# First layer of a hybrid decoder trunk: the opening reads a feature-major copy of x, and the first half's values get their token factor on the way out

## The chip, the cores and the metric

The kernel runs on one core of one Trainium2 chip. Its metric is the device time of one execution in microseconds (us), lower is better. The core has five engines that each work through their own instructions in order: TensorE (PE in the profile, its weight loads PEld), VectorE (DVE), ScalarE (ACT), GpSimd (POOL) and SyncE (SP), which issues most transfers.

## The reference

Two layers on 1024 tokens of 1024 features, all in f32. Cut to what matters here:

```python
def rmsnorm(x, g):
    y = x * lax.rsqrt(jnp.mean(x * x, axis=-1, keepdims=True) + RMS_EPS)
    return y * g

for l in range(DEPTH):                        # DEPTH = 2
    h = rmsnorm(x, norm1[l])
    proj = h @ w_in[l]                        # 1024 x 5120
    qa, ka, va, qb, kb, vb, gate_pre = jnp.split(proj, splits, axis=-1)
    o_a = dilated_mixture(qa, ka, va)         # 12 heads of sliding windows
    o_b = stick_breaking_attention(qb, kb, vb)   # 4 heads, causal
    gates = sigmoid(gate_pre + b_gate[l])
    merged = g_a * (o_a @ w_br[l, :256]) + g_b * (o_b @ w_br[l, 256:])
    x = x + merged @ w_o[l]
    ...                                       # a gated feed-forward with a 3-tap convolution
return rmsnorm(x, norm_f)
```

The normalized `h` is x times a factor for each token (one over the root of its mean square) times a gain for each feature.

## The kernel before

All activations lie feature-major in the on-chip memory: a tile has 128 features on its partitions and tokens along its rows. There are eight feature blocks (`KD`) and two halves of 512 tokens (`n`). Each f32 operand of a product is split into two parts, `hi` and `lo` (`hh`, `hl` for the normalized h, `w_hi`, `w_lo` for weights): ScalarE rounds to `hi`, VectorE subtracts to get `lo`, and TensorE does three matmuls, hi x hi, hi x lo and lo x hi (`product`, lines 188 to 190). The arguments of a matmul name its stationary operand and then its moving one.

The first layer opens with `first` (from line 2020) and `head` (from line 618). `first` reads x by token tiles of 128 tokens (`load`), squares them on ScalarE with a sum along the row, takes the root and the reciprocal (`scaled`), and turns each tile feature-major by eight TensorE transposes (`turned`, line 2054). The first two token tiles are scaled before they are turned (`in_two`); the other six are turned raw, copied out by ScalarE (`kept`, which also stores them to the DRAM tile `xs`), and scaled by eight VectorE instructions of 128 tokens, with the token factors spread over the partitions by another transpose (`normed`). The raw normalized h (`RAW`, `h_raw`) stays for later sums. `head` projects the stick-breaking values (`v_ps`, 256 columns of weights), keys (`kq_ps`) and queries (`q_ps`).

Behind the opening come the dense products of the layer (`i_a`, `i_b`, `i_c`), each over four feature blocks, in a fast-multiplication scheme that works on sums of quarters: `block_sums` (from line 1065) lets VectorE form these operand sums (`h_sum`, `h_raw`, line 1082 to 1091) and their splits (`t_hi`, `t_lo`), and for each weight tile the sums `in_a` and splits. Between them stand the attention items. One stick-breaking item (`stick_item`, line 707) has score matmuls `z`, ScalarE sigmoids `beta` and `stay`, a running product `stay` on VectorE (line 744), the product `beta` (line 751), transposes of `beta` on TensorE (`sb_t`, line 759) and matmuls with the values (`sb_o`).

TensorE's instructions stand in the order in which the program is written. In the opening ScalarE's and VectorE's order is written out too for the first steps, and left to the scheduler behind them, which orders instructions by its own estimates. Each engine then keeps its order: an instruction that waits holds all behind it on its engine. SP holds transfers in the same way.

## Time and profile before

| | us |
|---|---|
| median of 3 runs | 2603.27 |
| lowest to highest | 2602.32 to 2603.33 |
| the profiled execution | 2603.86 |
| its span on the core | 2602.2 |
| TensorE busy in the span | 2589.6 |
| VectorE busy | 2084.7 |
| ScalarE busy | 1349.5 |
| GpSimd busy | 105.6 |

Rows of a timeline give the start from the span's start, the time taken, engine, line, operation, output and inputs, shapes, and how many instructions in a row were merged; in brackets stands the idle time of the engine just before and what ended it. Instructions of one engine overlap at their ends, so the spacing of starts says more than the time of one. A row by stretches gives the busy time of each engine.

The opening's places in time: the first value matmul at 8.36, the first key matmul at 29.19, the first dense product at 65.39, the first score matmul of an attention item at 76.41.

### The profile page before, as it was taken

The numbers are of one execution on the slowest core, as the hardware profiler recorded it, in microseconds if no ns is written. First come the engines' busy times: TensorE is split into PE (matmuls) and PEld (weight loads), VectorE is DVE, ScalarE is ACT, GpSimd is POOL, SyncE is SP. The second block draws the span as 40 slices with busy tenths as digits, with TensorE's granted clock in tenths as the row PEclk, the third lists the DMA queues.
The fourth block names the chain that finished last, engine by engine and source line by source line (L and its number), as shares of the span: only waits on it lengthen the run. The fifth ranks groups of instructions, "written<-read, shape, count | busy, mean of one in ns | idle before, by whom it ended". The sixth has DMA issues, their size and how long they took to land.

```text
span 2602.2 us, 36060 instructions
## 1 busy us (share of the span) xinstructions
PE 2589.6 (100%) x12647; PEld 2165.4 (83%) x12647; DVE 2084.7 (80%) x3485; ACT 1349.5 (52%) x2521; POOL 105.6 (4%) x145
## 2 busy tenths in 40 slices
PE   9999999999999999999999999999999999999999
PEld 8888888888888888888888888888888888888887
DVE  8877777796888888897677788777869888889965
ACT  6555666664554545422445555666645555554225
POOL 3000000030000000000000000000300000000000
PEclk9999999999999999999999999999999999999999
DMA  7434578863244454688344436798633354447863
GB/s 257 152 119 134 163 207 226 236 235 101 88 148 157 138 176 134 243 325 311 146 147 146 128 127 194 194 235 238 198 99 121 122 171 136 154 162 264 342 242 118
DMA packets 401409, 470.60 MB, mean 181 GB/s; under 512 B 24500, under 2 KB 315980, under 8 KB 399436
## 3 DMA queue, kind: packets, MB, share of 16 engines
q1 hardware_dynamic: 400364, 465.90, 55.2%
q0 software_dynamic: 704, 2.13, 0.4%
q8 instruction: 100, 1.64, 0.3%
q14 instruction: 81, 0.66, 0.1%
q10 hardware_dynamic: 160, 0.27, 0.0%
HBM read 305.59 MB, written 162.63 MB: 180 GB/s over the span
## 4 chain that ended last, share of the span: by engine, by line
PE 93%; DVE 3%; ACT 2%; DMA 1%; issue 1%; SPq 0%; POOL 0%; DVEq 0%; ACTq 0%
PE u_a L1060 6%; PE u_a L1061 6%; PE u_a L1059 6%; PE d_ps L1823 5%; PE d_ps L1825 5%; PE d_ps L1824 5%; PE i_a L1059 5%; PE i_a L1060 5%; PE i_a L1061 5%; PE u_c L1059 3%; PE u_c L1060 3%; PE u_c L1061 3%; PE i_c L1059 2%; PE i_c L1061 2%; PE i_c L1060 2%; PE o_ps L188 2%
## 5 line engine op out<-in xcount | busy, mean ns | idle before, releaser
L146 ACT CAST w_hi<-up_a 128x512 fp32r<-128x512 f32 x280 | 174.0, 622 | 277.1 <-DVE up_a L1677 120.8
L154 DVE TENSOR_TENSOR w_lo<-up_a,w_hi 128x512 fp32r<-128x512 f32 x280 | 189.3, 688 | 83.6 <-ACT w_hi L146 83.6
L146 ACT CAST w_hi<-in_a 128x512 fp32r<-128x512 f32 x252 | 156.2, 622 | 161.8 <-PE i_c L1060 35.6
L154 DVE TENSOR_TENSOR w_lo<-in_a,w_hi 128x512 fp32r<-128x512 f32 x252 | 172.7, 687 | 73.3 <-ACT w_hi L146 64.7
L1834 DVE TENSOR_TENSOR x<-x,d_ps 128x512 f32<-128x512 f32 x220 | 149.9, 683 | 60.3 <-PE d_ps L1825 57.0
L1059 PE MATMUL u_a<-hh,w_hi 128*128 128x512 f32 x320 | 124.5, 389 | 0.0
L1060 PE MATMUL u_a<-hl,w_hi 128*128 128x512 f32 x320 | 124.5, 389 | 0.0
L1061 PE MATMUL u_a<-hh,w_lo 128*128 128x512 f32 x320 | 124.5, 389 | 0.0
L1059 PE MATMUL u_a<-t_hi,w_hi 128*128 128x512 f32 x320 | 124.5, 389 | 0.0
L1060 PE MATMUL u_a<-t_lo,w_hi 128*128 128x512 f32 x320 | 124.5, 389 | 0.0
L1061 PE MATMUL u_a<-t_hi,w_lo 128*128 128x512 f32 x320 | 124.5, 389 | 0.0
L1823 PE MATMUL d_ps<-gd_in,w_hi 128*128 128x512 f32 x316 | 123.2, 390 | 0.0
L1825 PE MATMUL d_ps<-gd_in,w_lo 128*128 128x512 f32 x316 | 123.0, 389 | 0.0
L1824 PE MATMUL d_ps<-gd_in,w_hi 128*128 128x512 f32 x316 | 122.9, 389 | 0.0
L1059 PE MATMUL i_a<-hh,w_hi 128*128 128x512 f32 x288 | 117.9, 410 | 0.0
L1059 PE MATMUL i_a<-t_hi,w_hi 128*128 128x512 f32 x288 | 116.5, 404 | 0.0
L1061 PE MATMUL i_a<-hh,w_lo 128*128 128x512 f32 x288 | 113.1, 393 | 0.0
L1061 PE MATMUL i_a<-t_hi,w_lo 128*128 128x512 f32 x288 | 113.1, 393 | 0.0
L1060 PE MATMUL i_a<-hl,w_hi 128*128 128x512 f32 x288 | 112.9, 392 | 0.0
L1060 PE MATMUL i_a<-t_lo,w_hi 128*128 128x512 f32 x288 | 112.9, 392 | 0.0
L1823 PE MATMUL d_ps<-gd_in,wd 128*128 128x512 f32 x284 | 111.0, 391 | 0.0
L1825 PE MATMUL d_ps<-gd_in,wd 128*128 128x512 f32 x284 | 110.5, 389 | 0.0
(405 smaller groups left out, 7738.7 us busy)
## 6 DMA issues: line engine op xcount, KB each, us to landing
gd<-g SPq DMA_DIRECT2D x154, 512.0 KB, 3.1
gd_in<-gd SPq DMA_DIRECT2D x154, 512.0 KB, 6.2
up_a<-in_w_up_dram SPq DMA_DIRECT2D x80, 512.0 KB, 5.5
in_a<-in_w_in_dram SPq DMA_DIRECT2D x72, 512.0 KB, 5.4
wd_raw<-in_w_down_dram SPq DMA_DIRECT2D x22, 1024.0 KB, 11.4
gin<-gs SPq DMA_DIRECT2D x32, 512.0 KB, 4.3
w_raw<-in_w_o_dram SPq DMA_DIRECT2D x64, 256.0 KB, 2.8
gs<-u SPq DMA_DIRECT2D x48, 256.0 KB, 2.5
```

What stands on the lines that cost most here:

```text
L146: one = act.copy(hi, src)
L154: two = dve.tensor_tensor(lo, src, f32(hi), ALU.subtract)
L188: pe.matmul(o, lh, rh, start=(first and i == 0), stop=False, skip_group_check=share)
L1059: pe.matmul(o, w[0][:, c], rh, start=(first and i == 0), stop=False, skip_group_check=True)
L1060: pe.matmul(o, w[0][:, c], rl, start=False, stop=False, skip_group_check=True)
L1061: pe.matmul(o, w[1][:, c], rh, start=False, stop=(last and i == 3), skip_group_check=True)
L1823: pe.matmul(o, wh[:, c], gh, start=(i == 0 and k in (0, 4, 5)), stop=False, skip_group_check=True)
L1824: pe.matmul(o, wh[:, c], gl, start=False, stop=False, skip_group_check=True)
L1825: pe.matmul(o, wl[:, c], gh, start=False, stop=(i == m - 1), skip_group_check=True)
L1834: dve.tensor_tensor(x, x, o, ALU.add)
```

## The change

Two inputs are added, both only laid out anew outside of the kernel: `xt`, x feature-major, and `gt0`, the first gain by feature block. `first` and the first layer's part of `head` become one new `first`:

- The first half's x is read feature-major straight into `RAW`. Its values are projected from x times the gain alone (`u_parts`), in chunks of two feature blocks, first for tokens 0 to 255, then 256 to 511. The value weights of chunks 0 and 1 are split on VectorE, those of 2 and 3 on GpSimd.
- The token factors come from squares of the feature-major x: ScalarE squares, TensorE sums over the partitions with a column of ones (`total`). Factors are applied to the first half's values when they leave PSUM (`scaled_values`).
- The first half's h is then scaled in place, 512 tokens at a time (`scale`, `rest`), with the key and query matmuls of a feature block right behind it.
- The second half's squares are taken from four token-major tiles by ScalarE (`whole`), its h is scaled the same way, its values are projected two feature blocks at a time, then its keys and queries.
- Nothing is stored to `xs` in the first layer; the later residual reads `xt` instead (`x_in`).
- 18 matmuls on a blank tile stand ahead of the first product, 3 on the identity before.

```diff
-WARM = 3
+WARM = 18
...
-def trunk_kernel(ctx, tc, x, norm1, w_in, b_gate, w_br, w_o, norm2, w_up, conv_w, conv_b, w_down, norm_f, out, depth=None, probe=None):
+def trunk_kernel(ctx, tc, x, xt, gt0, norm1, w_in, b_gate, w_br, w_o, norm2, w_up, conv_w, conv_b, w_down, norm_f, out, depth=None, probe=None):
...
+    blank = sb.tile([P, 512], F32, tag="pt", bufs=PT, name="blank")[:, 0:P]
+    pool.memset(blank, 0.0)
...
     def masks():
...
         pool.affine_select(t[2], t[1], [[1, 256]], ALU.is_ge, FAR, base=0, channel_multiplier=-1)
-        dve.tensor_copy(base0, t[2])
...
         pool.iota(rem, [[-1, 256]], base=256, channel_multiplier=1)
-        one = dve.tensor_scalar(rem, rem, 3, None, ALU.bitwise_and)
-        tc.add_manual_dep(one.ins, LAST["g0"], NO_SYNC, reason="in turn")
+        yield
+        dve.tensor_copy(base0, t[2])
+        dve.tensor_scalar(rem, rem, 3, None, ALU.bitwise_and)
...
-    def x_in(n, h):
+    def x_in(l, n, h):
...
-        nc.sync.dma_start(X[n][h], xs[n][:, 4 * h : 4 * h + 4, :])
+        src = xs[n][:, 4 * h : 4 * h + 4, :] if l else xt[:, 4 * h : 4 * h + 4, n * HF : (n + 1) * HF]
+        nc.sync.dma_start(X[n][h], src)
...
         else:
-            first_units = relay(head(l, dense))
...
+            opening = first(dense)
+            with tc.manual_schedule(engines={ET.Activation, ET.DVE, ET.Pool}):
+                next(opening)
             next(vectors)
-            for _ in first_units:
+            for _ in opening:
                 dense.aside()
...
-    def first():
...
+    def first(dense):
+        win = w_in[0].rearrange("(k p) n -> p k n", p=P)
+        nc.scalar.dma_start(g0, gt0)
+        warm = sb.tile([P, 8], F32, tag="ss", bufs=2, name="warm")
+        act.activation(warm[:, 0:1], eps, AF.Sqrt)
+        raw = big("w_raw").rearrange("p a (b c) -> p (a b) c", c=256)
+        raw_h(0)
+        raw_h(1)
+        new_h(0)
+        halves = [slice(0, 256), slice(256, HF)]
+        def xin0(q, t):
+            return RAW[0, q // 2][:, 2 * (q % 2) : 2 * (q % 2) + 2, t]
+        for q in range(4):
+            kk = slice(2 * q, 2 * q + 2)
+            nc.sync.dma_start(xin0(q, halves[0]), xt[:, kk, halves[0]])
+            nc.sync.dma_start(raw[:, kk, :], win[:, kk, OFF_VB : OFF_VB + 256])
+        for h in range(2):
+            nc.sync.dma_start(RAW[0, h][:, :, halves[1]], xt[:, 4 * h : 4 * h + 4, halves[1]])
+        wp = bank("t", "warm")
+        for _ in range(WARM):
+            pe.matmul(wp[:, 0:P], blank, blank, start=True, stop=True)
+        mask = masks()
+        next(mask)
+        wv = []
+        def w_parts(q):
+            hi = sb.tile([P, 2, 256], F32R, tag="wh", bufs=4, name="w_hi")
+            lo = sb.tile([P, 2, 256], F32R, tag="wl", bufs=4, name="w_lo")
+            src = raw[:, 2 * q : 2 * q + 2, :]
+            eng = dve if q < 2 else pool
+            eng.tensor_copy(hi, src)
+            one = eng.tensor_tensor(lo, src, f32(hi), ALU.subtract)
+            LAST["again"] = one.ins.name
+            wv.extend((hi[:, i, :], lo[:, i, :]) for i in range(2))
+        def u_parts(k, t):
+            x = RAW[0, k // 4][:, k % 4, t]
+            hi, lo = (y[:, k, t] for y in H[0])
+            act.mul(hi, x, g0[:, k : k + 1])
+            dve.scalar_tensor_tensor(lo, x, g0[:, k : k + 1], f32(hi), ALU.mult, ALU.subtract)
+        def square(q, t):
+            sq = small("sq").rearrange("p (a b) -> p a b", a=2)
+            act.activation(sq, xin0(q, t), AF.Square)
+            return sq
+        def v_step(m, q, o, j2=range(2)):
+            for part in range(3):
+                for k in (2 * q, 2 * q + 1):
+                    for m_, o_ in zip(m, o):
+                        for j in j2:
+                            t = 2 * m_ + j
+                            tok = slice(t % 4 * P, (t % 4 + 1) * P)
+                            left = h_part(t // 4, k)[part == 2][:, tok]
+                            pe.matmul(
+                                o_[:, j * 256 : (j + 1) * 256], left, wv[k][part == 1],
+                                start=(k == 0 and part == 0 and j == 0), stop=(k == KD - 1 and part == 2 and j == 1), skip_group_check=True,
+                            )
+        vt = new_v("vb")
+        ss = [sb.tile([P, 8], F32, tag="ss", bufs=2, name="ss") for _ in range(2)]
+        o1 = bank("ps", "v_ps")
+        acc = None
+        for q in range(4):
+            w_parts(q)
+            for k in (2 * q, 2 * q + 1):
+                u_parts(k, halves[0])
+            v_step([0], q, [o1])
+            sq = square(q, halves[0])
+            if acc is None:
+                acc = sq
+            else:
+                dve.tensor_tensor(acc, acc, sq, ALU.add)
+        wk, wq = kq_weights(0, pool)
+        xr = []
+        for i in range(4):
+            xr.append(sb.tile([P, T], F32, tag="p4", bufs=4, name="xr"))
+            nc.sync.dma_start(xr[i], xin[(4 + i) * P : (5 + i) * P, :])
+        for h in range(2):
+            nc.sync.dma_start(RAW[1, h], xt[:, 4 * h : 4 * h + 4, HF:T])
+        o2 = bank("ps", "v_ps")
+        tot = bank("t", "nrm_t")
+        def total(sq, c, first, last):
+            for a in range(2):
+                pe.matmul(tot[:, c : c + 1], sq[:, a, (c % 2) * P : (c % 2 + 1) * P], ones, start=(first and a == 0), stop=(last and a == 1), skip_group_check=True)
+        sqs = {}
+        for q in range(4):
+            for k in (2 * q, 2 * q + 1):
+                u_parts(k, halves[1])
+            sqs[q] = square(q, halves[1])
+            v_step([1], q, [o2])
+            if q == 1:
+                for c in range(2):
+                    total(acc, c, True, True)
+            if q > 1:
+                for c in (2, 3):
+                    total(sqs[q - 2], c, q == 2 and c == 2, False)
+        for q in (2, 3):
+            for c in (2, 3):
+                total(sqs[q], c, False, q == 3)
+        def factors(n, src):
+            act.activation(ss[n][:, 0:4], src, AF.Sqrt, bias=eps[:, 0:1], scale=1.0 / D)
+            dve.reciprocal(ss[n][:, 4:8], ss[n][:, 0:4])
+        def across(n):
+            rb = bank("o", "nrm_b")
+            for c in range(4):
+                pe.transpose(rb[:, c * P : (c + 1) * P], ss[n][:, 4 + c : 5 + c].to_broadcast([P, P]), ident)
+            return rb
+        def scale(n, k, rb):
+            h_ = RAW[n, k // 4][:, k % 4, :]
+            dve.scalar_tensor_tensor(h_, h_, g0[:, k : k + 1], rb, ALU.mult, ALU.mult)
+            act.copy(H[n][0][:, k, :], h_)
+        def rest(n, k):
+            LAST["h"] = dve.tensor_tensor(H[n][1][:, k, :], RAW[n, k // 4][:, k % 4, :], f32(H[n][0][:, k, :]), ALU.subtract).ins.name
+        def scaled_values(m, o):
+            for j in range(2):
+                t = 2 * m + j
+                f = ss[0][:, 4 + t : 5 + t]
+                ov = o[:, j * 256 : (j + 1) * 256].rearrange("p (h c) -> p h c", h=4)
+                vv = vt[0][:, :, t, :]
+                act.mul(vv[:, :, 0:64], ov, f)
+                dve.scalar_tensor_tensor(vv[:, :, 64:128], ov, f, f32(vv[:, :, 0:64]), ALU.mult, ALU.subtract)
+        def keep_v(h):
+            LAST["sv"] = nc.sync.dma_start(sv[0][:, :, 4 * h : 4 * h + 4, :], f32(vt[h])).ins.name
+        def kq_step(c, k, o, n):
+            (wh, wl), (xh, xl) = (wk, wq)[c][k], h_part(n, k)
+            pe.matmul(o, wh, xh, start=(k == 0), stop=False)
+            pe.matmul(o, wh, xl, start=False, stop=False)
+            pe.matmul(o, wl, xh, start=False, stop=(k == KD - 1))
+        def kq_out(c, n, o):
+            hi, lo = small("kq_h", F32R), small("kq_l", F32R)
+            LAST["head"] = [x.name for x in in_parts(c, SCALE, hi, lo, o)]
+            LAST["pair"] = LAST["head"][0]
+            keep_kq(c, n, 0, hi, lo)
+        def whole(i):
+            sq = xr[i]
+            act.activation(sq, xr[i], AF.Square, accum_out=ss[1][:, i : i + 1])
+        next(mask)
+        factors(0, tot[:, 0:4])
+        rb = across(0)
+        o = [bank("s", "kq_ps"[c:]) for c in range(2)]
+        scale(0, 0, rb)
+        for k in range(KD):
+            if k + 1 < KD:
+                scale(0, k + 1, rb)
+            rest(0, k)
+            for c in range(2):
+                kq_step(c, k, o[c], 0)
+            if k in (1, 2):
+                scaled_values(k - 1, (o1, o2)[k - 1])
+            if k == 2:
+                keep_v(0)
+            if k >= 3 and k < 7:
+                whole(k - 3)
+        factors(1, ss[1][:, 0:4])
+        table(AF.Sigmoid, ss[1][:, 4:5])
+        rb = across(1)
+        new_h(1)
+        scale(1, 0, rb)
+        dense.prime(1)
+        ov = [bank("ps", "v_ps") for _ in range(2)]
+        for k in range(KD):
+            if k + 1 < KD:
+                scale(1, k + 1, rb)
+            rest(1, k)
+            if k % 2:
+                v_step([2, 3], k // 2, ov)
+            if k in (1, 3):
+                kq_out(k // 2, 0, o[k // 2])
+        yield
+        for m in (2, 3):
+            o = ov[m - 2].rearrange("p (j h c) -> p h j c", j=2, h=4)
+            vv = vt[1][:, :, 2 * (m % 2) : 2 * (m % 2) + 2, :]
+            act.copy(vv[:, :, :, 0:64], o)
+            dve.tensor_tensor(vv[:, :, :, 64:128], o, f32(vv[:, :, :, 0:64]), ALU.subtract)
+        keep_v(1)
+        dense.done.add("wv")
+        for c in range(2):
+            yield from kq_half(c, (wk, wq)[c], 1, "s")
...
+    xt = np.asarray(inputs["x"])[0].T.reshape(KD, P, T).transpose(1, 0, 2)
+    inputs = {**inputs, "xt": xt, "gt0": np.asarray(inputs["norm1"])[0].reshape(KD, P).T}
```

TensorE's order behind the five small transposes of `setup` is the same in both programs. On the other engines instructions move; three places matter. The names: `w_raw` raw value weights, `w_hi`, `w_lo` their parts, `kq_w` split key and query weights, `h_raw` the normalized h and, in place, its sums.

GpSimd, from the masks to the key and query weights. Before:

```order
L102 IOTA rem 128x256
L2047 TENSOR_TENSOR w_lo<-w_raw,w_hi 128x512 x2
L176 CAST kq_w<-w_raw 128x512 x2
L177 TENSOR_TENSOR kq_w<-w_raw,kq_w 128x512 x2
L2120 TENSOR_TENSOR h_raw<-hh_194,hl_195 128x256 x4
```

And now:

```order
L103 IOTA msk 128x256
L2036 CAST w_hi<-w_raw 128x512
L2037 TENSOR_TENSOR w_lo<-w_raw,w_hi 128x512
L2036 CAST w_hi<-w_raw 128x512
L2037 TENSOR_TENSOR w_lo<-w_raw,w_hi 128x512
L179 CAST kq_w<-w_raw 128x512
L180 TENSOR_TENSOR kq_w<-w_raw,kq_w 128x512
```

Two casts of value weights moved here from ScalarE, and the sums that rebuilt `h_raw` are gone.

ScalarE, while the first half's h is scaled, now (`xr` are the second half's token tiles, squared with a sum into `ss`):

```order
L2124 CAST hh_123<-h_raw 128x512
L2155 ACTIVATE xr,ss<-xr 128x1024
L2124 CAST hh_123<-h_raw 128x512
L2155 ACTIVATE xr,ss<-xr 128x1024
L2124 CAST hh_123<-h_raw 128x512
L2155 ACTIVATE xr,ss<-xr 128x1024
L2124 CAST hh_123<-h_raw 128x512
L2155 ACTIVATE xr,ss<-xr 128x1024
L2112 ACTIVATE ss<-ss,eps 128x4
```

The four row squares stand between the casts of the last four feature blocks; before, eight such squares were spread over the token tiles.

VectorE ahead of the first attention item. Before:

```order
L154 TENSOR_TENSOR hl_195<-h_raw,hh_194 128x512 x2
L1223 TENSOR_TENSOR u<-u,i_c 128x512
L154 TENSOR_TENSOR w_lo<-in_a,w_hi 128x512
L744 SCALAR_TENSOR_TENSOR stay<-stay,over 128x512
L751 TENSOR_TENSOR beta<-beta,stay 128x512
L606 TENSOR_TENSOR u<-u,in_a 128x512
L744 SCALAR_TENSOR_TENSOR stay<-stay,over 128x512
L1229 TENSOR_TENSOR u_926<-u_926,i_a 128x512
L751 TENSOR_TENSOR beta<-beta,stay 128x512
```

And now:

```order
L157 TENSOR_TENSOR hl_124<-h_raw,hh_123 128x512
L1180 TENSOR_TENSOR in_a<-in_a 128x512
L157 TENSOR_TENSOR hl_124<-h_raw,hh_123 128x512
L1222 TENSOR_TENSOR u_804<-u_804,i_a 128x512
L157 TENSOR_TENSOR w_lo<-in_a,w_hi 128x512
L610 TENSOR_TENSOR u<-u,in_a 128x512
L157 TENSOR_TENSOR hl_124<-h_raw,hh_123 128x512
L1183 TENSOR_TENSOR in_a<-in_a 128x512
L157 TENSOR_TENSOR hl_124<-h_raw,hh_123 128x512
L737 SCALAR_TENSOR_TENSOR stay<-stay,over 128x512 x2
L744 TENSOR_TENSOR beta<-beta,stay 128x512 x2
```

Sums and splits for the next weight tile moved ahead of the running products, and the two `beta` now stand last.

201 lines of the change are left out of this document (20 added, 181 removed).

## The prediction

> **What bounds the kernel now.** I read the page first, then the stretches of the opening, then who waits for whom around its end. The page's busy times and chain:
>
> ```profile
> PE 2589.6 (100%) x12647; PEld 2165.4 (83%) x12647; DVE 2084.7 (80%) x3485; ACT 1349.5 (52%) x2521; POOL 105.6 (4%) x145
> PE 93%; DVE 3%; ACT 2%; DMA 1%; issue 1%; SPq 0%; POOL 0%; DVEq 0%; ACTq 0%
> ```
>
> TensorE (PE) is busy for the whole span, so a change is worth the TensorE time that it takes out or the TensorE idle time that it puts in. Next the busy times by stretch (PE, PEld, DVE, ACT, POOL, then clock, DMA share, GB/s):
>
> ```profile
> 0.00:8.40 8.40, 6.33 (x34) 5.79 (x34) 3.92 (x12) 4.72 (x9) 2.83 (x15) 1.00 0.70 230
> 8.40:25.30 16.90, 15.79 (x127) 14.54 (x126) 12.92 (x33) 16.22 (x35) 10.80 (x12) 1.00 0.89 297
> 25.30:41.90 16.60, 16.58 (x96) 14.39 (x97) 16.29 (x46) 11.81 (x23) 8.03 (x8) 1.00 0.92 299
> 41.90:65.40 23.50, 23.50 (x153) 21.14 (x151) 19.91 (x33) 10.98 (x20) 0.00 (x0) 1.00 0.62 204
> 65.40:83.20 17.80, 17.80 (x81) 14.35 (x79) 16.52 (x30) 14.07 (x30) 1.01 (x3) 1.00 0.49 151
> 83.20:110.00 26.80, 26.80 (x137) 22.28 (x136) 25.00 (x42) 14.02 (x28) 0.83 (x2) 1.00 0.59 185
> ```
>
> TensorE idles 3.2 us in all, before 25.3. VectorE (DVE) is the tight one behind it: 16.3 of 16.6 us, then 19.9 of 23.5, then 16.5 of 17.8. The timelines mark three places:
>
> ```profile
> 41.83 1.28 DVE L1082 TENSOR_TENSOR h_sum<-h_raw 128x512 f32<-128x512 f32 x2
> 65.39 0.50 PE L1059 MATMUL i_a<-hh,w_hi 128*128 128x512 f32 x1
> 82.56 0.68 DVE L751 TENSOR_TENSOR beta<-beta,stay 128x512 f32<-128x512 f32 x1
> 83.29 0.20 PEld L759 LDWEIGHTS sb_t<-ident,beta 128*128 128x128 f32 x2 [0.23 <-DVE beta L751]
> ```
>
> At 41.83 VectorE has normalized and split all 1024 tokens and begins the operand sums of the dense products. At 65.39 the opening's matmuls are done and the dense products begin. At 83.29 TensorE loads the first attention item's weights and has **waited 0.23 us for VectorE's beta**, which ends at 83.24. So VectorE is already the last to arrive there: whatever moves that beta moves everything behind it. The last two stretches above show TensorE full from 65.4 to 110, and the built order shows that its instructions behind the vectors' transposes are the same in both kernels, and VectorE's are the same again from about the second attention item.
>
> **The change part by part.** TensorE loses 80 transposes of x and gains 20 column sums; the rows:
>
> ```profile
> 10.39 1.04 PE L2054 MATMUL x_t<-ident,xr 128*128 128x128 f32 x8
> 628.63 0.94 PE L539 MATMUL nrm_t<-ones,nrm 128*128 128x1 f32 x8
> 12.71 0.28 PE L190 MATMUL v_ps<-w_hi,hl 128*128 128x256 f32 x1
> 12.83 0.28 PE L188 MATMUL v_ps<-w_hi,hh 128*128 128x256 f32 x1
> 40.19 0.39 PE L188 MATMUL q_ps<-hh,kq_w 128*128 128x512 f32 x1
> 40.42 0.39 PE L189 MATMUL q_ps<-hl,kq_w 128*128 128x512 f32 x1
> ```
>
> A transpose is (1.04 - 0.27)/7 = 0.11 us, so 8.8 us go. A column sum in f32 is two records 0.11 apart (the first row groups four sums as eight records), so 20 cost 4.5. Value matmuls are 0.12 apart, key/query matmuls 0.23; the opening's useful work stays 192 x 0.12 + 96 x 0.23 = 45.1. TensorE alone would gain about 4 us. What decides is when VectorE gets through, so I follow it to that beta.
>
> *First 256 tokens' values.* They need xt and the weights in four chunks of 0.52 MB, 2.1 MB in all. The rate and two landings:
>
> ```profile
> 2.00:10.00 8.00, 7.52 (x42) 6.77 (x43) 5.52 (x14) 5.72 (x12) 1.47 (x5) 1.00 0.94 322
> 7.09 0.62 ACT L2041 CAST w_hi<-w_raw 128x512 fp32r<-128x512 f32 x1 [0.72 <-DMA w_raw<-in_w_in_dram]
> 11.64 1.06 ACT L2063 ACTIVATE xsq<-xr 128x1024 f32<-128x1024 f32 x1 [0.32 <-DMA xr<-in_x_dram]
> 10.88 2.53 POOL L2047 TENSOR_TENSOR w_lo<-w_raw,w_hi 128x512 fp32r<-128x512 f32 x2 [7.41 <-ACT w_hi L2041]
> 13.83 0.61 POOL L176 CAST kq_w<-w_raw 128x512 fp32r<-128x512 f32 x1 [0.42 <-DMA w_raw<-in_w_in_dram]
> ```
>
> At 322 GB/s from 2.0 us the 1.05 MB up to the first of these landings would be there at 5.3, the 2.6 MB of the second at 10.1: landings come 1.6 us behind the rate. So chunk 3 lands at 8.5, chunk 4 at 10.1. Their weights are split by GpSimd (POOL): a cast (0.6) and a subtraction (1.27), one chunk after the other: 10.4 and 12.2. The eight matmuls behind end the first part at **13.2** (bounds: 11.8 if GpSimd is not late, 14.5 if 1 KB rows move slower).
>
> *Second 256 tokens* and the sums: 48 x 0.12 + 4.5 = 10.3, to **23.5**. *Factors:* sums, square root, reciprocal, transposes, first scaling, as in a later norm:
>
> ```profile
> 629.61 0.26 ACT L541 ACTIVATE ss<-nrm_t,eps 128x4 f32<-128x4 f32 x1 [0.35 <-PE nrm_t L539]
> 629.90 0.18 DVE L542 RECIPROCAL ss<-ss 128x4 f32<-128x4 f32 x1
> 636.38 0.60 PE L548 MATMUL nrm_b<-ident,ss 128*128 128x128 f32 x4
> 637.01 1.41 DVE L556 SCALAR_TENSOR_TENSOR b_f<-x,g,nrm_b 128x512 f32<-128x512 f32 x2 [0.63 <-PE nrm_b L548]
> ```
>
> That is 0.3 + 0.3 + 0.2 + 0.6 = 1.4: VectorE starts scaling at **24.9**.
>
> *Keys and queries of the first half.* Per feature block VectorE does one scaling (1.41/2, 0.67 apart) and one subtraction, 0.61 apart as in
>
> ```profile
> 40.45 1.46 DVE L154 TENSOR_TENSOR hl<-h_raw,hh 128x512 fp32r<-128x512 f32 x2
> 17.23 1.08 ACT L2063 ACTIVATE xsq<-xr 128x1024 f32<-128x1024 f32 x1
> 18.44 0.29 ACT L2066 ACTIVATE ss<-ss,eps 128x1 f32<-128x1 f32 x1
> ```
>
> 8 x 1.28 = 10.2, four value scalings of 256 columns at 0.36 = 1.4, 0.6 of waits for ScalarE's halves of these. The four row squares (1.2 each, 17.23 to 18.44) stand between ScalarE's casts of blocks 4 to 7, and hold the last subtraction by 1.4; the last square, root, reciprocal and transposes add 1.8 before the second half may be scaled. Sum 15.4, to **40.3** (14.2 to 15.7). *Second half:* 10.2, two key/query remainders 1.2, waits for their ScalarE halves 0.6: 12.0, to **52.3** (11.3 to 12.6). Before, VectorE was here at 41.83.
>
> *To the beta.* In the old program 61 VectorE instructions stand from the first h_sum to that beta; 35.6 us of work by their spacings (busy rows above: 19.9 + 16.5), the rest of 41.4 idle. In the new order 63 stand there: one key/query remainder fewer, one w_lo and two in_a sums more, so 36.8. Inside it the key remainder waits for TensorE's second-half keys, 24 x 0.23 = 5.5 after the last value matmul: VectorE reaches it 3.9 us after 52.3, it is ready 6.0 after; about 2 us idle. **52.3 + 38.8 = 91.1** against 83.24: **+7.9**. Bounds: 36.8 with no idle, 42.6 with as much as before (5.8).
>
> TensorE follows the second half's values by 0.5, does 11.0 of keys and queries and 0.7 of vectors, begins the dense products at 64.5 and would be at the beta 17.8 later, at 82.3: it waits there some 9 us. Nothing gives that back, since TensorE is full behind it. The profiled execution took 2603.86 (span 2602.2), its forecast is 2611.8; the median 2603.27 lies 0.6 under it, so **2611.2**. Extremes of all bounds: 11.8 + 10.3 + 1.4 + 25.5 + 36.8 = 85.8 (+2.6) to 14.5 + 10.3 + 1.4 + 28.3 + 42.6 = 97.1 (+13.9).
>
> Hidden at nothing: the masks' six VectorE rows (1.7 us, 3.8 to 5.4 before) now stand ahead of the reciprocal, under the last value step; uncovered they cost 1.7. The 4 MB not written to xs: TensorE never waited on it. Key/query weights 3 and 4 wait on SP for GpSimd (about 14 and 16) with two x rows and xt's second half queued behind them: 3.5 MB, there by 28, wanted at 33 to 40.
>
> *A rule against this change.* GpSimd now does twelve casts and subtractions of 128x512 from 8.5 to 21, while VectorE forms remainders from two SBUF inputs:
>
> ```profile
> L154 DVE TENSOR_TENSOR hl<-h_raw,hh x12: 675/692/1242, 19.3 to 41.2; 128x512 fp32r<-128x512 f32 x12
> 17.73 3.29 POOL L2120 TENSOR_TENSOR h_raw<-hh,hl 128x256 f32<-128x256 f32 x4
> 19.28 2.29 DVE L154 TENSOR_TENSOR hl<-h_raw,hh 128x512 fp32r<-128x512 f32 x2
> ```
>
> The two at 19.28, under GpSimd, are 0.5 us longer each than the median. 14 VectorE rows meet GpSimd in the new order; I count none of it in the sum, since TensorE paces that stretch; at 0.5 each, 7 us on 6 of work, they would end about 2 us behind TensorE. The Trainium skill (SBUF — State Buffer, Who interferes with whom) has an exclusive lock: a VectorE instruction with two SBUF inputs and a GpSimd one that reads SBUF block each other for the whole instruction; this agrees with the row.
>
> **The rivals.** (1) *VectorE does not decide* (the other side): its sums are ready when TensorE wants them. For it: in the old trace nothing but 0.23 us waits there. Against: that wait shows no slack at all, and 63 rows at 0.6 do not fit into 30 us. Then TensorE's own path counts: 24.9 + 1.3, keys/queries 11.0, 1.5 of factors, values 11.5, keys/queries 11.0, vectors 0.7 = 61.9 for 65.39: -3.5, **2599.8**. It decides if VectorE needs under 30 us from there to the beta instead of 38.8. (2) *GpSimd and VectorE block each other*: +2 to +2.5 on the sum, **2613.5**. (3) *TensorE comes back slow from its long wait.* At the start its f32 records are twice as long:
>
> ```profile
> 3.92 1.97 PE L2143 MATMUL gb<-ident,g 128*128 128x128 f32 x8 [0.26 <-DVE g L2140]
> ```
>
> 0.22 apart, against 0.11 at 10.39. The clock column reads 1.00 there, so it does not show it. Against: later gaps are too short to tell. A wait of some 9 us before the beta could bring such a start again; the old one lasted from 1.8 to about 6, so up to 2 us: **2613**. The Trainium skill (TensorE: Matmul & The Clock Gate, The HAM clock gate) halves the clock after about 3.4 us idle, for as long again: 1.7 by it.
>
> **How the numbers follow.** About 0.2% (5.2 us) is what can be told from no change: below 2598.1, above 2608.5. The forecast, VectorE late at the beta by its bounds, 0.54, own range 2606 to 2616; 0.13 of it under 2608.5. Rival 1 0.26, of which 0.10 under 2598.1 (bounds 1 to 3 us better), the rest within. Rivals 2 and 3 0.10 each, slower. Faster 0.10, same 0.13 + 0.16 = 0.29, slower 0.41 + 0.20 = 0.61. Range 2599 to 2616.
>
> **What would show it.** Right: a TensorE wait of several us for beta (L744) between 75 and 91, second-half subtractions (L2127) ending near 52, L2036 on GpSimd ending near 12, nrm_t sums of 2.7 us in a row before the roots. Wrong: the dense products beginning under 60 with no wait behind them; then the VectorE account fails, at the opening or at the idle time I left in it.

## The result and the profile after

The changed kernel takes **2644.91 us** (median of 4, 2642.67 to 2647.14) against 2602.80 (2602.21 to 2603.33) for the kernel before on the same chip: a ratio of **1.016, 95% interval 1.0148 to 1.0172**. Slower, as forecast, but by 42 us where 8 were forecast. The profiled execution took 2642.67 with a span of 2640.7, against 2603.86 and 2602.2: 38.5 us more of span.

The page of the changed kernel, busy times and chain of waits:

```profile
PE 2616.1 (99%) x12620; PEld 2166.6 (82%) x12620; DVE 2099.8 (80%) x3465; ACT 1346.0 (51%) x2513; POOL 108.7 (4%) x140
PE 94%; DVE 3%; ACT 1%; issue 1%; DMA 1%; SPq 0%; ACTq 0%; DVEq 0%
```

TensorE idles 24.6 us, 12.0 more than before, and is *busy* 26.5 us longer although the change takes work from it. So there are two losses: idle time, and matmuls that take longer. The same stretches of the opening as before (PE, PEld, DVE, ACT, POOL, clock, DMA share, GB/s):

```profile
8.40:25.30 16.90, 15.02 (x112) 13.43 (x111) 16.90 (x20) 7.49 (x17) 14.09 (x13) 1.00 0.86 286
25.30:41.90 16.60, 13.54 (x56) 10.57 (x56) 12.25 (x24) 8.24 (x17) 0.00 (x0) 0.79 0.48 161
41.90:65.40 23.50, 20.54 (x136) 18.12 (x135) 18.06 (x29) 12.66 (x22) 0.00 (x0) 1.00 0.49 150
65.40:83.20 17.80, 16.45 (x73) 12.76 (x72) 15.48 (x30) 10.84 (x21) 0.00 (x0) 1.00 0.65 210
83.20:110.00 26.80, 20.68 (x86) 15.95 (x85) 26.68 (x42) 16.14 (x34) 9.92 (x4) 0.87 0.20 71
```

TensorE is idle in every one of them, where it had been full from 25.3 on, and the granted clock falls to 0.79 and 0.87 in two. The places that the prediction named, from the timelines of VectorE and TensorE:

```profile
58.97 2.49 DVE L1075 TENSOR_TENSOR h_sum<-h_raw 128x512 f32<-128x512 f32 x4
73.09 0.50 PE L1052 MATMUL i_a<-hh,w_hi 128*128 128x512 f32 x1
98.31 1.26 DVE L744 TENSOR_TENSOR beta<-beta,stay 128x512 f32<-128x512 f32 x2
99.02 1.29 PE L752 MATMUL sb_t<-ident,beta 128*128 128x128 f32 x3 [4.69 <-DVE beta L744]
```

The h_sums begin at 58.97 (52.3 forecast), the dense products at 73.09 (64.5), and TensorE waits for beta, but 4.69 us instead of some 9.

From before the first attention item on, both kernels give TensorE the same matmuls in the same order, so each can be set against itself. How much later one and the same matmul runs (its *lateness*), by its time in the kernel before:

| time before, us | 83.3 (first sb_t) | 98.8 | 188 | 643 | 1096 | 1968 | 2596.5 (last) |
|---|---|---|---|---|---|---|---|
| later in the changed kernel, us | 16.3 | 18.7 | 19.2 | 20.9 | 27.0 | 30.7 | 38.0 |

**16.3 us** are lost up to the first beta, **2.4** in the 15 us behind it, and **19.3** over the rest, where nothing was changed. The last shows in a stretch far from the opening, the kernel before first, the changed one second:

```profile
700.00:900.00 200.00, 200.00 (x883) 165.28 (x882) 169.87 (x256) 101.80 (x164) 0.00 (x0) 1.00 0.44 150
```

```profile
700.00:900.00 200.00, 200.00 (x871) 163.10 (x870) 171.53 (x263) 102.19 (x166) 0.00 (x0) 1.00 0.40 134
```

Both are busy for 200.00 us at a clock of 1.00, but 12 records fewer fit into the same time. No wait, clock or busy share tells it; the count does, and so does the mean time of one product. By form (count, busy us, mean ns), products of the feed-forward, with the normalized rows (hh) or sums of them (t_hi) as moving operand:

```profile
L1052 PE MATMUL u_a<-hh,w_hi 128*128 128x512 f32 x320 | 126.7, 396 | 0.0
L1052 PE MATMUL u_a<-t_hi,w_hi 128*128 128x512 f32 x320 | 124.5, 389 | 0.0
```

```profile
L1059 PE MATMUL u_a<-hh,w_hi 128*128 128x512 f32 x320 | 124.5, 389 | 0.0
```

In the changed kernel (first two rows) products with hh as moving operand take 396 ns, those with t_hi 389; before (last row) hh had 389 too. Only some operands are slow. What is special to them is their **place in SBUF**. Tiles get places in the order in which they are first taken. The changed code takes the 4-byte tile `junk` (in `table`, to load the sigmoid's table) ahead of `new_h(1)`, the old code behind it. It occupies 32 bytes, so the second half's hh and hl start at byte 192864 and 209248 of a partition instead of 192832 and 209216, and gd_in uses these places later. The weights w_hi and w_lo stay where they were modulo 512. In the built program, 3312 of the 10056 products with 512 columns now have moving operand and weights at different places modulo 256 bytes; before, none had. That these are the slow ones was a theory to be tested.

### The profile page after: what moved, and what is told of

It is laid out like the page before. It is cut to its first block, busy times and chain, and to the rows that moved or that the text cites. A ratio compares the mean times of both kernels' runs of the same rounds, so it can differ in the third digit from the quotient of the medians.

```text
span 2640.7 us, 35957 instructions
## 1 busy us (share of the span) xinstructions
PE 2616.1 (99%) x12620; PEld 2166.6 (82%) x12620; DVE 2099.8 (80%) x3465; ACT 1346.0 (51%) x2513; POOL 108.7 (4%) x140
## 4 chain that ended last, share of the span: by engine, by line
PE 94%; DVE 3%; ACT 1%; issue 1%; DMA 1%; SPq 0%; ACTq 0%; DVEq 0%
PE u_a L1052 6%; PE u_a L1054 6%; PE u_a L1053 6%; PE d_ps L1805 5%; PE d_ps L1807 5%; PE d_ps L1806 5%; PE i_a L1052 5%; PE i_a L1053 5%; PE i_a L1054 5%; PE u_c L1052 3%; PE u_c L1054 3%; PE u_c L1053 3%; PE i_c L1052 2%; PE i_c L1054 2%; PE i_c L1053 2%; PE o_ps L191 2%
## 5 line engine op out<-in xcount | busy, mean ns | idle before, releaser
L1816 DVE TENSOR_TENSOR x<-x,d_ps 128x512 f32<-128x512 f32 x220 | 150.2, 684 | 64.5 <-PE d_ps L1807 60.7
```

Source lines behind the costliest of these rows:

```text
L1816: dve.tensor_tensor(x, x, o, ALU.add)
```

## The experiments

### Is it the place? Eight kernels that move tiles and change no instruction

Each adds an unused tile, widens `junk` or takes it later; the order on every engine is that of the kernel it starts from. Behind each median stand the ratio to the kernel before on the same chip and its 95% interval. First, the changed kernel with a wider `junk` (64 bytes), and the kernel before with the second half's operands, or with everything, 32 bytes further:

```diff
 # e1_after_pad (from the changed kernel)
-        junk = sb.tile([P, 1], F32, tag="junk", name="junk")
+        junk = sb.tile([P, 16], F32, tag="junk", name="junk")[:, 0:1]
 # e2_before_h1_off (from the kernel before)
             if c == 0:
+                if n == 1:
+                    sb.tile([P, 1], F32, tag="gap", name="gap")
                 new_h(n)
 # e3_before_all_off (from the kernel before)
     g0 = cp.tile([P, KD], F32, name="g0")
+    cp.tile([P, 1], F32, name="gap")
```

> The changed kernel with one tile made wider: the one-column junk tile that the table switch writes gets 16 columns (64 bytes a partition, not 4), so that hh1 and hl1 behind it in SBUF start at a multiple of 64 bytes again (192896, not 192864); no instruction and no order changes. Address theory: the 38.4 us came in two parts, 18.7 us by 110 us into the program and 19.3 us spread evenly over the rest, and the second part is the 3264 matmuls whose moving operand starts 32 bytes off (234 ns apart, not 227) and the few behind each. Then the spacing goes back to 227 ns, the drift stays near 18.7 us after 110 us, and the time is 2621 us by the profile and 2622 to 2626 us in the median. Clock theory: TensorE is slowed for the rest of the run by something that the late opening leaves behind (a mean granted clock of 0.997): 2643 to 2647 us as before. Traffic theory: the slow matmuls collide with transfers that the change moved: 2643 to 2647 us too, since no transfer moves.

> The kernel before with an unused 4-byte tile taken ahead of hh1, which pushes hh1 and hl1 32 bytes up (from 192832 to 192864); the instructions and their order are the same. Address theory: its dense products on the second half of the tokens slow from 227 to about 234 ns, with the same count of matmuls as in the changed kernel: 2602 + 19 to 22 = 2621 to 2625 us. Clock and traffic theories: nothing in the opening or the transfers changes, 2602 to 2604 us.

> The kernel before with an unused 4-byte tile among the constants, which pushes every working tile 32 bytes up: all 10056 matmuls with 512 columns then read a moving operand that starts 32 bytes off a multiple of 64, and their stationary operands are off too. Address theory with a price per matmul: 10056 x 7 to 8 ns = 70 to 80 us more, 2673 to 2683 us. A rival within it, that only the change between offset and unoffset tiles costs (a bank or row that two operands share): little or nothing, 2602 to 2610 us. A rival that an offset stationary operand costs as well: more than 2690 us.

Measured: e2 **2623.92** (1.0085, 1.0070 to 1.0100), e3 **2602.69** (1.0000, 0.9990 to 1.0009), e1 **2634.61** (1.0125, 1.0108 to 1.0142). So 32 bytes ahead of one operand, with no other edit, cost the old kernel 21 us; 32 bytes ahead of all cost nothing. It is the distance between operands, not the absolute place. The count in 700 to 900 us agrees, e2 first, then e3:

```profile
700.00:900.00 200.00, 200.00 (x872) 163.22 (x871) 168.80 (x255) 102.91 (x166) 0.00 (x0) 1.00 0.43 145
```

```profile
700.00:900.00 200.00, 199.99 (x882) 165.28 (x881) 169.92 (x256) 101.77 (x164) 0.00 (x0) 1.00 0.44 150
```

In e1, 64 bytes did not cure it; it only took a third of the loss behind the opening (12.3 us of 19.3 are left behind the matmul of 98.8 us). Which distances are harmless was then tried.

```diff
 # f1_before_weights_off (from the kernel before): the weights alone, 32 bytes
+            if r == 0:
+                sb.tile([P, 8], F32, tag="gap0", name="gap0")
             hi = sb.tile([P, 2, 256], F32R, tag="wh", bufs=4, name="w_hi")
             lo = sb.tile([P, 2, 256], F32R, tag="wl", bufs=4, name="w_lo")
+            if r == 0:
+                sb.tile([P, 24], F32, tag="gap1", name="gap1")
 # f3_before_h1_96 and g2_before_h1_256: as e2 with [P, 24] and [P, 64]
 # f2_after_pad128: as e1 with [P, 32]
 # g1_after_h1_first (from the changed kernel)
+        new_h(1)
         table(AF.Sigmoid, ss[1][:, 4:5])
         rb = across(1)
-        new_h(1)
```

> The kernel before with 32 unused bytes ahead of the split-weight buffers w_hi and w_lo and 96 behind them, so that only these stand 32 bytes higher and every other tile stays at its place modulo 128 bytes; order of instructions unchanged. All tiles off together cost nothing, hh1 alone cost 19 to 21 us, so an offset as such is not what costs. Pair theory: a matmul is slow when its moving operand and the weights that are loaded for the next one start at different places modulo 128 bytes, whichever of the two was moved. Then 8484 of the 10056 matmuls with 512 columns are slow, at the second experiment's 19.3 us for 3264 (5.9 ns each): 50 us, 2648 to 2658 us. Rival: hh1 and hl1 stood wrong to something else (the other halves hh0 and hl0, what VectorE and ScalarE read and write): nothing, 2601 to 2606 us.

> The kernel before with a 96-byte unused tile ahead of hh1, so that hh1 and hl1 start 96 bytes past the weights' place modulo 128, that is 32 bytes behind it and not ahead. Pair theory: if only the distance counts, as with 32 bytes ahead, 2621 to 2625 us; if the order counts, anything between nothing (2602 us) and that.

> The kernel before with a 256-byte unused tile ahead of hh1 and hl1. If the places must agree modulo 256 bytes, nothing is lost: 2601 to 2604 us. If modulo 512, the loss is like that at 128 bytes (16 us behind the opening in the changed kernel): 2614 to 2620 us.

> The changed kernel with the junk tile 32 columns wide (128 bytes a partition), so that hh1 and hl1 stand at 64 modulo 128 bytes as the weights do; no instruction changes. With 16 columns they stood 64 bytes apart from the weights and still lost 12.3 us after 110 us, against 19.3 us at 32 bytes apart. Pair theory: now nothing is lost behind the opening, the drift stays at 18.7 us, 2621 us by the profile, 2621 to 2624 us in the median. Rival, that something else of the change slows TensorE too: 2627 us or more.

> The changed kernel with the tiles hh1 and hl1 taken ahead of the table switch's junk tile, so that they start at byte 192832 as in the kernel before; order and instructions unchanged. The wide junk tile (128 bytes) left hh1 equal to the weights modulo 128 and the matmuls were still slow, so the two places must agree over a longer stretch: in the kernel before all pairs agree modulo 512, in the runs with losses they differ by 32, 64, 96 and 128. Pair theory, so mended: no loss behind the opening, the drift stays at 18.7 us, 2621 us by the profile, 2621 to 2624 us in the median (an opening in which the clock falls once more, as in the run with 128 bytes, would add 4). Rival, that the change slows TensorE by something beside the places: 2627 us or more.

| kernel | moving operand minus weights, modulo 256 bytes (products) | median us | cost of the distance, us |
|---|---|---|---|
| e3 (all by 32) | 0 | 2602.69 | none |
| g2 (256 bytes) | 0 | 2603.69 | none (1.0003, 0.9993 to 1.0012) |
| e2 | 32 (3312) | 2623.92 | 21 |
| f3 | 96 (3312) | 2625.47 | 22.5 |
| f1 | 96 (5412), 224 (3072), 128 (1056), 160 (36) | 2650.80 | 47.8 |
| the changed kernel | 32 (3312) | 2644.91 | 19.3 behind 98.8 us |
| e1 | 64 (3312) | 2634.61 | 12.3 behind 98.8 us |
| f2 | 128 (3312) | 2642.80 | 16.7 behind 98.8 us |
| g1 | 0 | 2624.07 | none: lateness 18.2 at 98.8, 17.9 at the end |

The products are counted by their own weights; 48 of each 3312 lie the same distance the other way (224 for 32). The weights of the next product, which are loaded meanwhile, lie at the same distance in nearly all, so the runs don't tell which of the two matters. f1 moved the weights by 32 bytes and the tiles behind them by 128. Its expectation counts distances modulo 128; modulo 256 there are four of them, and 9576 of its 10056 products are apart.

A mismatched product costs 5 to 7 ns: 21.2/3312 = 6.4, 22.5/3312 = 6.8, 47.8/9576 = 5.0. The starts in the traces say the same: two products in a row start 227 ns apart in the median where the places agree, and 230 (64 apart, e1) to 234 (32 apart) where they don't. In f1 nearly all products are slow, those with t_hi too, and f1 has the fewest records in its stretch; in g1 hh has its 389 ns back:

```profile
L1059 PE MATMUL u_a<-t_hi,w_hi 128*128 128x512 f32 x320 | 126.7, 396 | 0.0
700.00:900.00 200.00, 200.00 (x858) 160.91 (x858) 166.44 (x252) 100.13 (x161) 0.00 (x0) 1.00 0.42 140
```

```profile
L1052 PE MATMUL u_a<-hh,w_hi 128*128 128x512 f32 x320 | 124.5, 389 | 0.0
700.00:900.00 200.00, 200.00 (x882) 165.33 (x881) 172.09 (x265) 102.68 (x166) 0.00 (x0) 1.00 0.42 140
```

That settles the cause of the larger half: taking the operands ahead of `junk` gives 21 us back (2644.91 to 2624.07). Why the chip cares is not shown. In its profiled execution f2 lost 4 us more in the opening than the changed kernel (20.6 against 16.3 at the first sb_t), though nothing in it was moved but places; there the granted clock fell in one more spell:

```profile
19.00:22.00 3.00, 2.62 (x14) 0.65 0.61 193
22.00:25.00 3.00, 3.00 (x16) 0.50 0.93 313
```

The places don't explain this spell: f4 below has the same places and the same instructions up to 27 us, and its clock is 1.00 from 7 to 28. It seems to be a matter of the single execution: the mean clock of f2's four ranges from 0.995 to 0.998.

### What does GpSimd cost VectorE?

e4 starts from e1, keeps GpSimd out of the opening's splits (VectorE splits the value weights, ScalarE and VectorE those of keys and queries) and drops one dependence of a GpSimd memset.

```diff
-            eng = dve if q < 2 else pool
+            eng = dve
...
-        wk, wq = kq_weights(0, pool)
...
+        def more(n):
+            wkq.append(weights(w_in[0][:, (OFF_KB, OFF_QB)[n] :][:, 0:P], P, place_w(1, "kq_w")))
...
+            if q % 2:
+                more(q // 2)
```

> The first experiment's kernel with GpSimd out of the opening: the last two value-weight splits go to VectorE, the key and query weights to ScalarE (high parts) and VectorE (low parts), placed between the second 256 tokens' pieces; their loads keep their place. Blocking theory: VectorE's rows took twice as long while GpSimd worked (128x256 subtractions 0.92 us against 0.43, sums of squares 1.09 to 1.77 against about 0.6), some 8 us in all between 8.4 and 24 us, more than the 5 us of rows that VectorE gains here; the column sums end near 24.5 us, not 27.3, and the end comes 2 to 3 us earlier than in the first experiment, 2618 to 2619 us by the profile. Rival, that VectorE's own work bounds this stretch: no gain, or 1 to 2 us lost, 2621 to 2623 us.

Measured: **2630.58** (1.0112, 1.0097 to 1.0127), 4.0 under e1, though the ranges just overlap (2629.29 to 2634.56 against 2634.17 to 2635.27); at the matmul of 98.8 us e4 is 3.2 us earlier (15.5 late, e1 18.7). Rows of VectorE, GpSimd and TensorE from the timeline of the changed kernel, then of VectorE and TensorE from that of e4:

```profile
12.01 1.77 DVE L2079 TENSOR_TENSOR sq<-sq 128x512 f32<-128x512 f32 x1
15.50 7.39 DVE L2045 SCALAR_TENSOR_TENSOR hl<-h_raw,g,hh 128x256 fp32r<-128x256 f32 x8
20.52 1.34 POOL L180 TENSOR_TENSOR kq_w<-w_raw,kq_w 128x512 fp32r<-128x512 f32 x1
24.61 2.73 PE L2093 MATMUL nrm_t<-ones,sq 128*128 128x1 f32 x24
```

```profile
11.47 0.68 DVE L2078 TENSOR_TENSOR sq<-sq 128x512 f32<-128x512 f32 x1
14.53 1.67 DVE L2044 SCALAR_TENSOR_TENSOR hl<-h_raw,g,hh 128x256 fp32r<-128x256 f32 x4
21.93 2.73 PE L2093 MATMUL nrm_t<-ones,sq 128*128 128x1 f32 x24
```

Eight remainders of 256 columns take 0.92 us each beside GpSimd and 0.42 without it, a sum of squares 1.77 against 0.68, and the column sums end at 27.34 against 24.66. The Trainium skill (SBUF — State Buffer, Who interferes with whom) states a lock for such a pair, a VectorE row that reads two SBUF tensors and a GpSimd row that reads SBUF; the runs agree, with rows about twice as long. It works the other way too. A mask of beta on GpSimd, 0.3 to 0.4 us in the kernel before, takes in the changed kernel

```profile
93.45 3.85 POOL L723 TENSOR_SCALAR_AFFINE_SELECT beta<-beta 128x128 f32<-128x128 f32 x1 [0.58 <-ACT beta L717]
```

beside VectorE rows that follow each other without a pause. This mask is for a later item and does not hold up the first beta.

### What does the clock cost?

In the changed kernel TensorE's clock by 3 us windows (PE busy, clock, DMA):

```profile
28.00:31.00 3.00, 1.36 (x6) 0.76 0.67 245
31.00:34.00 3.00, 3.00 (x8) 0.50 0.00 0
97.00:100.00 3.00, 0.85 (x4) 0.64 0.00 0
100.00:103.00 3.00, 3.00 (x9) 0.50 0.26 89
```

It is at half once behind the one-column sums and the short waits at the factors, and once from the end of the wait for beta on. Matmuls with no use, whose results nothing reads, were put into these gaps: f4 is f2 with 4, 12 and 32 of them, g3 is g1 with 2, 7 and 20. The edit of g3:

```diff
+    def fill(o, n):
+        for _ in range(n):
+            pe.matmul(o, ident, ident, start=True, stop=True, skip_group_check=True)
...
             tp = bank("t", "sb_t")
+            if "filled" not in LAST:
+                LAST["filled"] = fill(tp[:, 0:P], 20)
...
+        fill(tot[:, 256:384], 2)
...
+        fill(o[0][:, 0:P], 7)
```

> The kernel with the 128-byte junk tile, and filler matmuls (128x128, ident on ident, into banks that are overwritten) in TensorE's three waits of the opening: 4 behind the column sums, 12 behind the first spread of the factors, 32 ahead of the first sb_t transposes. Clock theory: the granted clock fell to 0.50 from 30 to 33 us and from 99 to 105 us, where matmuls stood 0.43 us apart and not 0.23, because TensorE had had little to do; with the fillers it stays at 1.00, the 2.3 us behind the first sb_t are saved and perhaps some of the 2.8 us at 30 us, 2616 to 2619 us by the profile against 2621. Rival: the clock falls all the same, or the fillers hold up the transposes: 2620 to 2624 us.

> hh1 taken first, and the fillers of the run before at about half their number (2, 7 and 20): one filler takes 0.2 us, not 0.1, so that the 48 ran past the waits they were to fill. Clock theory: the granted clock stays at 1.00 around the first sb_t, and the 2.3 us lost behind it are saved, 2618 to 2619 us by the profile against 2621. Rival: the 2.3 us come back as a later wait, 2621 us.

Measured: f4 2642.54 against f2's 2642.80, g3 **2624.24** (1.0082, 1.0067 to 1.0097) against g1's 2624.07. Each filler takes 0.2 us, so f4's were too many: its clock holds at the first sb_t, but at the matmul of 98.8 us it is 19.5 us late, where the changed kernel with its half clock is 18.7. In g3 the clock holds there too:

```profile
96.00:99.00 3.00, 3.00 (x30) 1.00 0.26 100
99.00:102.00 3.00, 2.48 (x14) 1.00 0.17 68
```

and its last matmul is 16.5 us late where g1's is 17.9, but the medians do not show this gain. The four executions of g3 fall into two pairs: 2621.5 and 2622.3 us at a mean granted clock of 0.999, 2626.2 and 2626.4 at 0.997. So the fillers seem to have held the clock in two of four; where it fell in the others is not on record. The clock costs 2.4 us in the changed kernel's trace (the rise from 16.3 to 18.7 in the table of lateness; g3 rises by 0.1), and that as a saving was not confirmed by times.

### All three together, and what is left

g4 takes g1's order of tiles, e4's splits and g3's fillers.

> All three remedies on the changed kernel: hh1 taken first, no GpSimd splits in the opening, fillers in the waits. If the three prices add up (19.3 us, 3.1 us, and what is left of the clock's, 1 to 2 us): 2602.2 + 18.7 - 3.1 - 1 to 2 = 2616 to 2617 us by the profile, still 14 us behind the kernel before, because VectorE's rows of the opening are untouched. If they do not add up: 2619 to 2624 us.

Measured: **2618.47** (1.0060, 1.0045 to 1.0075): 26.4 of the 42 us are back, 15.6 are left. By the profile it is 2616.4, as the three prices add up to. Three kernels ask what the rest is. h1 takes eight VectorE rows, the second half's remainders, away (their low parts are zero instead, written by ScalarE); h2 lets ScalarE scale the first half's values one step earlier, square the token rows and take the second half's factors two steps earlier, so that VectorE waits less for them; h3, from h2, lets the operand sums of the dense products go as soon as they can instead of behind the key remainders, and leaves out the 20 fillers.

```diff
 # h1_less_dve (from g4)
-            rest(1, k)
+            act.mul(H[1][1][:, k, :], f32(H[1][0][:, k, :]), 0.0)
 # h2_reordered (from g4)
+            if k in (0, 1):
+                scaled_values(k, (o1, o2)[k], False)
...
-            if k >= 3 and k < 7:
-                whole(k - 3)
-        factors(1, ss[1][:, 0:4])
+            if k >= 1 and k < 5:
+                whole(k - 1)
+            if k == 5:
+                factors(1, ss[1][:, 0:4])
 # h3_sums_free (from h2)
-                LAST["filled"] = fill(tp[:, 0:P], 20)
...
         def behind(one, eng=1):
-            tc.add_manual_dep(one.ins, LAST["head"][eng], NO_SYNC, reason="behind")
+            if l:
+                tc.add_manual_dep(one.ins, LAST["head"][eng], NO_SYNC, reason="behind")
```

> The kernel with all three remedies (2616.4 us by the profile), in which ScalarE instead of VectorE writes the low parts of the second half's normalized input, as zeros: the low parts are left out of the result, and VectorE has 8 rows of 0.61 us less between 43 and 57 us, 4.9 us. If VectorE's rows set the end of the opening: 2611 to 2612 us by the profile. If its waits for ScalarE do (its rows alternate with the casts, and ScalarE gets 8 more): between that and 2616 us. If another engine does: 2616 us.

> The kernel with all three remedies, with VectorE's rows unchanged and some of its waits taken away: ScalarE scales the high parts of the first half's values one step earlier (VectorE waited four times 0.5 us for them), squares the token rows two steps earlier and takes the second half's factors two steps before the first half ends (VectorE waited 0.7, 0.9 and 1.1 us there). If these waits were on the path: up to 4.5 us less, 2612 to 2614 us by the profile. If they only move behind the next cast: 2616 us. The kernel before stays ahead in either case.

> The reordered kernel (2616.5 us by the profile, 12.7 us late behind the first sb_t), in which the sums of block rows no longer stand behind the key product's row in the first layer: six of them (3.6 us) move ahead of VectorE's 3.65 us wait for it. The 20 fillers ahead of the first sb_t go, since the wait they filled should shrink from 4.7 to about 1 us. Queue theory: the rows that were ready behind that wait are now done in it, the first beta and the first sb_t come 3.6 us earlier, the drift behind them is about 9 us, and the time is 2612 to 2613 us by the profile. Rival, that TensorE or ScalarE set the beta: 2616 to 2618 us.

Measured: h1 2619.71 (1.0063, 1.0048 to 1.0078), h2 **2616.82** (1.0052, 1.0035 to 1.0069), h3 2619.96 (1.0061, 1.0045 to 1.0078). The key remainder of the second half in g4, in h1 and in h2:

```profile
66.03 0.69 DVE L615 TENSOR_TENSOR kq_l<-kq_ps,kq_h 128x512 fp32r<-128x512 f32 x1 [3.65 <-ACT kq_h L614]
```

```profile
66.88 0.69 DVE L615 TENSOR_TENSOR kq_l<-kq_ps,kq_h 128x512 fp32r<-128x512 f32 x1 [4.42 <-ACT kq_h L614]
```

```profile
64.12 0.69 DVE L615 TENSOR_TENSOR kq_l<-kq_ps,kq_h 128x512 fp32r<-128x512 f32 x1 [3.65 <-ACT kq_h L614]
```

Five us of VectorE work less in h1 brought nothing: VectorE waits longer for the key product and ends no earlier than in g4. So VectorE's work alone does not decide in 43 to 57 us. But h1 gave ScalarE eight rows more, and so does not show what decides in g4: TensorE, ScalarE, or the three by turns. h2 is 2 us earlier than g4 at the matmul of 98.8 us (12.8 late against 14.7), but in its profiled execution not at the end (14.3 against 14.1); its median is 1.7 lower with overlapping ranges (2616.37 to 2618.33 against 2617.20 to 2619.33), so its worth is not settled. In h3 TensorE gets the first beta 1.6 us earlier than in h2 (93.84 against 95.41), but without fillers it waits 4.71 for it, and the clock is at half behind:

```profile
93.84 1.29 PE L756 MATMUL sb_t<-ident,beta 128*128 128x128 f32 x3 [4.71 <-DVE beta L748]
96.00:99.00 3.00, 3.00 (x8) 0.50 0.18 69
```

The slow spell takes back what the earlier beta gave: at the matmul of 98.8 us h3 is 13.4 late, h2 12.8. At the end it is 16.4 against 14.3, and 1.8 of that is one later wait that h2 does not have, between 700 and 800 us:

```profile
PE u_c L1056 <- ACT u L1683: 1.8, 1, 1.8
```

So the order of VectorE's queue from 61 us on was on the path at the first beta, and freeing it was worth 1.6 us there, of 3.6 expected, and nothing in the total. No version beat the kernel before.

## Why the prediction was right or wrong

The sign and the first mechanism were right: the new opening brings the first beta later, TensorE waits for it there, and what is lost there stays lost (in g1, 18.2 us at the matmul of 98.8 us and 17.9 at the end). The size was wrong by 34 us, by the profile 38.5 for 7.9, in three steps.

**"Nothing gives that back, since TensorE is full behind it"** was read as *the same order behind the opening takes the same time*. This is the step that failed most: **19.3 us** of the 38.5. The built order was the same; the places of its operands were not, and 3312 products took about 6 ns more each. Neither the order nor the profile of the kernel before can show this; the places in the built program do.

**The sum to the beta**, 91.1, came out at 99.5. By its terms:

| term | forecast | measured | off | what the trace shows |
|---|---|---|---|---|
| to the end of the column sums | 23.5 | 27.3 | +3.8 | GpSimd and VectorE slow each other; e4 takes 2.7 of it back |
| first half's factors, keys, queries, to the second half's scaling | 16.8 | 18.7 | +1.9 | VectorE waits four times 0.5 for ScalarE's halves of the values, 0.6 in all forecast |
| second half | 12.0 | 12.9 | +0.9 | two waits of 0.6 for ScalarE's kq_h, 0.6 in all forecast |
| first h_sum to beta | 38.8 | 40.6 | +1.8 | 2 us idle forecast, 3.7 in one wait for kq_h |

The last, in the changed kernel, with the ready sums queued behind it:

```profile
57.59 1.46 DVE L2127 TENSOR_TENSOR hl<-h_raw,hh 128x512 fp32r<-128x512 f32 x2
67.58 0.69 DVE L610 TENSOR_TENSOR kq_l<-kq_ps,kq_h 128x512 fp32r<-128x512 f32 x1 [3.71 <-ACT kq_h L609]
```

So behind the column sums VectorE's work was about right, and the error lies in **waits counted too small or as nothing**. The forecast let TensorE follow VectorE by 0.5; in fact the two wait for each other by turns. TensorE's waits in the opening (total, times, longest):

```profile
PE sb_t L752 <- DVE beta L744: 4.7, 1, 4.7
PE v_ps L2060 <- ACT hh L2124: 3.0, 3, 1.5
PE kq_ps L2143 <- ACT hh L2124: 1.6, 1, 1.6
PE v_ps L2060 <- DVE hl L2045: 1.4, 3, 1.0
```

TensorE came to the beta 12 us later than forecast (94.3 for 82.3), which is why its wait there was 4.7 and not 9. The measured 99.5 lies outside even the extreme of all bounds, 97.1. The waits for ScalarE, which the forecast put at 0.6 in each half, were the term to bound wider.

One more thing stands ahead of the beta, and no run took it away: the order of VectorE's rows. The two first running products read what ScalarE had written by 89.9 and 92.4, but VectorE comes to them at 96.0, behind remainders and sums of the dense products and without an idle moment:

```profile
91.77 0.62 ACT L718 ACTIVATE stay<-z 128x512 f32<-128x512 f32 x1
96.00 2.38 DVE L737 TENSOR_TENSOR_SCAN stay<-stay,over 128x512 f32<-128x512 f32 x2
```

In the kernel before, VectorE waited 0.23 us for ScalarE at the first of them. An estimate from these rows is that up to 3.6 of the 4.7 us of TensorE's wait lie in this order; h3 has the same gap. It is untested.

**The half clock**: 2.4 us behind the wait, which the forecast left to a rival. What the earlier spell, at 30 us, costs is not shown; VectorE's waits there are for ScalarE, not for TensorE.

*The rivals.* The blocking (2) came true in addition to the forecast, at 2.7 us for the +2 to +2.5 of its estimate; counting it at nothing "since TensorE paces that stretch" was wrong: TensorE's value matmuls waited 1.4 us for the slowed remainders (the last of its waits above) and 0.4 for GpSimd's weights, and the column sums stand behind these matmuls in its order. The slow return (3) came true too, 2.4 us for "up to 2". The Trainium skill (TensorE: Matmul & The Clock Gate, The HAM clock gate) has a window of about 3.4 us for both, the idleness and the half clock behind it. The granted clock here is 0.50 from 29.6 to 36.4 and from 97.8 to 104.6, 6.8 us each, twice that window, and in g3 from 28.2 to 31.6, once; the measured spells decide. The second began 3.5 us into the wait for beta, as the Trainium skill has it. The first came behind 2.7 us of one-column sums and waits of 0.6 and 1.6 us, not behind 3.4 us of idleness. "VectorE does not decide" (1) was half right in its mechanism, as h1 shows for VectorE's work in 43 to 57 us, and wrong in its time: TensorE, which this rival put at 61.9 for its first dense product, came to it at 73.09. These three were alternatives in the forecast's chances; two of them added up with it.

*The signs.* L2036 on GpSimd ended at 11.8 (12 forecast), the nrm_t sums took 2.73 in a row (2.7): right. The second half's L2127 ended at 59.0 (52) and the wait for beta stood at 94.3 to 99.0, not between 75 and 91: right in kind, late in place. None of them could show the operands' places; the number of records in equal stretches does.

**Still open**: the mechanism behind the places; the 14 us of the opening that h2 leaves, VectorE's order ahead of the running products among them; what h2 is worth at the end.

## What to carry to other kernels

Taking one small tile earlier can move every tile behind it: after a change, compare the places of the matmul operands in the built program, not only the order of instructions, and where a stretch that wasn't touched grows, count the records in equal windows, for neither the busy share nor the clock shows it. Put small scratch tiles behind the large operands, or fix the operands' places relative to the weights. And where two engines hand work to each other block by block, give the sum a term for the waits of each, and add up the small losses that can occur together instead of treating them as alternatives.

## What the runs showed of the hardware

- A 512-column product runs 5 to 7 ns slower (such products follow each other at 230 to 234 ns in the median instead of 227) where its moving operand and its weights start at different places modulo 256 bytes: kernels with 3312 to 9576 of them, 32, 64, 96, 128 or 224 apart, lost 12 to 48 us; 0 and 256 lost nothing (e1, e2, e3, f1, f2, f3, g1, g2). The granted clock reads 1.00 and TensorE 100% busy meanwhile, in 700 to 900 us of each.
- The granted clock fell to 0.50 behind one-column sums and two short waits (29.6 to 36.4), and 3.5 us into a wait (97.8 to 104.6). Two kernels with the same instructions and places up to 27 us, f2 and f4, had a spell at 20 to 27 us in one and none in the other.
- 128x256 VectorE remainders took 0.92 us beside GpSimd's casts and subtractions and 0.42 without; a 128x128 mask on GpSimd took 3.85 us beside VectorE's rows and 0.3 to 0.4 in the kernel before.
